# The first products of two MLPs by one level of Strassen's algorithm, and the hidden tiles in four batches of eight

## The chip, the core and the metric

The kernel runs on one core of a Trainium2 chip. The metric is the time of one execution on the device in microseconds (us). The kernel before was timed three times: 1258.25, 1260.36 and 1261.16 us, median 1260.36. One more execution was profiled; the profile and the trace that are quoted here are of that one.

The engines are named as in the profile: PE is TensorE, which multiplies matrices, and PEld its loads of weights; DVE is VectorE, ACT is ScalarE, POOL is GpSimd, and SP is SyncE, which issues nearly all transfers from memory.

## What is computed

Two residual layers on 512 tokens of 1024 features, in float32. Each layer is a mixer (layer 0: convolution and a gated recurrence; layer 1: an attention without softmax) and an MLP with 4096 hidden features. The change touches the MLPs alone; this is the end of each layer in the reference:

```python
shift1, scale1, gate1, shift2, scale2, gate2 = jnp.split(mod[:, None, :], 6, axis=-1)
...
x = x + gate1 * y
h = rms_norm(x, norm_mlp[layer]) * (1.0 + scale2) + shift2
x = x + gate2 * (jnp.square(jax.nn.relu(h @ mlp_w1[layer])) @ mlp_w2[layer])
```

`mod` is the product of a vector with `ada_w` (the "adaLN" numbers: 6 x 1024 for each layer). The kernel works them out beside the other work, and this matters for the order below.

## The kernel before

**Tiles.** Everything lies with the features on the 128 partitions and the 512 tokens along the row. So `h` is eight tiles of 128 x 512 (`hT`), the hidden layer is 32 such tiles, and the output eight.

**Three matmuls for one.** A float32 number is held as a high part, rounded to the format that TensorE takes (fp32r), and a low part, the rest. `mm3` (L288) multiplies high by high, high by low and low by high: three matmuls for each 128 x 128 block of weights. For h the parts are `hh` and `hl`, for the hidden tiles `hidh` and `hidl`, for weights `whi` and `wlo`. Hidden tiles and weights are split by ScalarE (a cast gives the high part) and VectorE (a difference gives the low one).

**Weights.** One weight tile is 128 x 1024 float32, 512 KB: the eight blocks of one hidden tile, or eight blocks of a second-product tile. `raw_w` (L268) loads it by SP into one of three raw buffers; `split_w` makes the parts in one of four `whi` and four `wlo` buffers. SP takes its transfers in order, each when its buffer is free.

**The MLP** (`mlp`, L1002). The hidden tiles are worked in two halves of sixteen. In each half, sixteen first products (24 matmuls of 512 columns each, then relu, square and split in `relu2`, L1006) are followed by the second product: eight output tiles o, each of two weight tiles (48 matmuls of 512 columns), and `x_add` (L508), which adds the result to x. In the second half the outputs 5, 6 and 7 are done in halves of 256 tokens, and the second part of their sums is left to be done after the loop, beside the next norm. `mlp_head` (L1065) does the first three hidden tiles of an MLP in halves of 256 tokens, since the norm of x, and so h, is ready in halves; for layer 1 a copy of it stands in the code of the attention (L1536 and after).

**Work in the background.** `background(n)` (L450) loads n tiles of `ada_w` through the same raw buffers and multiplies each with the vector on VectorE (`ada_dot`, a row `ascr<-wraw,cb`; I call it a dot). In layer 0's MLP two dots follow each hidden tile from the seventh on, and three each output tile of the first half, until none are left.

**What sets the order.** PE's order is that of the code. In the MLPs a scheduler of the language places the instructions of the other engines, each in one order that is fixed in the program; in the attention, and at the start of layer 1's MLP, a planner in the kernel (`Graph`, L110) does it from estimated times. An engine works its instructions strictly in order: one that waits holds up all behind it.

## Time and profile before

| what | before |
|---|---|
| median of three runs | 1260.36 us |
| the profiled execution | 1262.38 us |
| its span in the profile | 1260.6 us |
| granted TensorE clock, mean | 0.997 |
| matmuls in the trace, all | 6809 |
| of 512 columns with h against whi (L291) | 560 |
| of 512 columns with hidden tiles (by each of L291 to L293, with those of 256) | 576 |
| layer 0's MLP begins at | 268.0 us |

A line of a group reads: code line, engine, operation, result<-operands, shape, number of them, then busy time in us, mean length of one in ns, and after the second bar how long the engine had been idle ahead of them and what ended it. A line of the timeline reads: start in us, length in us, engine, line, operation, what, and in brackets the idle time ahead of it. A line of the windows reads: stretch of time, its length, busy time of PE, PEld, DVE, ACT and POOL with the number of instructions begun or running, then the granted clock, the share of the DMA engines and GB/s. A line of transfers ends with the median time in us from issue to landing. [...]

### The profile page before, as it was taken

Reading aid. Unit: us, or ns where it says so; the run is one execution under the profiler, and the core shown is the slowest. Engines: PE = TensorE matmul, PEld = TensorE weight load, DVE = VectorE, ACT = ScalarE, POOL = GpSimd, SP = SyncE. Lnnn points to the kernel's source line nnn. Section 1 sums busy time; section 2 is a strip of 40 time slices with the busy share of each in tenths; the row PEclk is TensorE's granted clock in tenths of the full one; section 3 lists DMA queues with packets and bytes.
Section 4 is the critical chain, followed back from the end, with each engine's and each line's share of the span. In section 5 each row is a group of like instructions: output and inputs, shape, how many; then the busy total and the mean of one; then the engine's idle time right before and its main releaser. Section 6 shows DMA issues by size and latency. Waiting matters only on the chain.

```text
span 1260.6 us, 17038 instructions
## 1 busy us (share of the span) xinstructions
PE 1240.0 (98%) x6809; PEld 1038.2 (82%) x6809; DVE 716.9 (57%) x1107; ACT 541.8 (43%) x891; POOL 12.2 (1%) x24
## 2 busy tenths in 40 slices
PE   7999999999999999999999999999999999999998
PEld 6788877898878888888987778777988888888888
DVE  8897868576666655433567774669753322333321
ACT  4333233355441143622458755667565421355210
POOL 0000000000000000000200000000000000000000
PEclk9999999999999999999999999999999999999999
DMA  8665443416776667332332213323132233222330
GB/s 301 229 211 169 150 151 100 134 35 214 243 247 227 220 205 233 129 97 88 101 101 68 67 53 99 84 68 101 35 101 90 95 100 101 98 89 97 117 109 25
DMA packets 46606, 163.35 MB, mean 130 GB/s; under 512 B 5296, under 2 KB 6328, under 8 KB 46528
## 3 DMA queue, kind: packets, MB, share of 16 engines
q1 hardware_dynamic: 46384, 161.78, 39.4%
q8 instruction: 53, 0.87, 0.3%
q10 hardware_dynamic: 144, 0.49, 0.1%
q14 instruction: 25, 0.20, 0.0%
HBM read 155.96 MB, written 2.10 MB: 125 GB/s over the span
## 4 chain that ended last, share of the span: by engine, by line
PE 86%; DMA 5%; DVE 5%; ACT 3%; issue 1%; SPq 0%; DVEq 0%; ACTq 0%
PE b L291 20%; PE b L292 20%; PE b L293 20%; DMA wraw<-in_w 4%; PE acc L291 3%; PE acc L293 3%; PE acc L292 3%; PE b L1382 2%; PE b L1403 1%; PE b L1438 1%; PE b L1302 1%; ACT whi L281 1%; DVE wlo L282 1%; DVE ascr L422 1%; PE b L1439 1%; PE b L1440 1%
## 5 line engine op out<-in xcount | busy, mean ns | idle before, releaser
L281 ACT CAST whi<-wraw 128x1024 fp32r<-128x1024 f32 x150 | 157.7, 1053 | 450.2 <-PE b L292 262.8
L282 DVE TENSOR_TENSOR wlo<-wraw,whi 128x1024 fp32r<-128x1024 f32 x150 | 183.4, 1224 | 244.2 <-ACT whi L281 241.4
L291 PE MATMUL b<-hh,whi 128*128 128x512 f32 (+1 forms) x720 | 266.9, 371 | 2.0 <-ACT hh L1262 1.1
L293 PE MATMUL b<-hh,wlo 128*128 128x512 f32 (+1 forms) x720 | 262.3, 365 | 0.0
L292 PE MATMUL b<-hl,whi 128*128 128x512 f32 (+1 forms) x720 | 262.2, 365 | 0.0
L291 PE MATMUL b<-hidh,whi 128*128 128x512 f32 (+1 forms) x576 | 207.5, 360 | 1.6 <-ACT hidh L300 1.6
L292 PE MATMUL b<-hidl,whi 128*128 128x512 f32 (+1 forms) x576 | 207.7, 361 | 1.3 <-DVE hidl L301 1.3
L293 PE MATMUL b<-hidh,wlo 128*128 128x512 f32 (+1 forms) x576 | 207.5, 360 | 0.2 <-DVE wlo L282 0.2
L291 PEld LDWEIGHTS b<-hh,whi 128*128 128x128 f32 x720 | 135.1, 188 | 30.6 <-issue 7.2
L293 PEld LDWEIGHTS b<-hh,wlo 128*128 128x128 f32 x720 | 135.0, 188 | 22.1
L292 PEld LDWEIGHTS b<-hl,whi 128*128 128x128 f32 x720 | 135.1, 188 | 21.6 <-DVE hl L1264 0.5
L422 DVE CUSTOM_DVE_ANT_0 ascr<-wraw,cb 128x1024 bf16<-128x1024 f32 x80 | 97.7, 1222 | 46.5 <-DMA wraw<-in_ada 45.9
L292 PEld LDWEIGHTS b<-hidl,whi 128*128 128x128 f32 x576 | 109.1, 189 | 18.2 <-DVE hidl L301 1.6
L291 PEld LDWEIGHTS b<-hidh,whi 128*128 128x128 f32 x576 | 108.5, 188 | 18.4 <-ACT hidh L300 2.0
L293 PEld LDWEIGHTS b<-hidh,wlo 128*128 128x128 f32 x576 | 108.5, 188 | 16.8 <-DVE wlo L282 0.6
L508 DVE SCALAR_TENSOR_TENSOR x<-b,modc,x 128x512 f32<-128x512 f32 (+1 forms) x70 | 44.8, 641 | 96.1 <-PE b L293 95.9
L1216 DVE TENSOR_TENSOR wlo<-raw,whi 128x1024 fp32r<-128x1024 f32 x33 | 40.3, 1222 | 30.1 <-ACT whi L1215 29.9
L301 DVE TENSOR_TENSOR hidl<-relu,hidh 128x512 fp32r<-128x512 f32 (+1 forms) x64 | 42.4, 665 | 23.4 <-ACT hidh L300 23.2
L291 PE MATMUL acc<-hh,whi 128*128 128x512 f32 x128 | 52.2, 408 | 0.0
L293 PE MATMUL acc<-hh,wlo 128*128 128x512 f32 x128 | 50.0, 390 | 0.0
L292 PE MATMUL acc<-hl,whi 128*128 128x512 f32 x128 | 49.9, 390 | 0.0
L1366 DVE TENSOR_TENSOR_SCAN om<-om,pat 128x772 f32<-128x772 f32 (+2 forms) x24 | 46.5, 1936 | 5.8 <-ACT om L1362 5.8
(335 smaller groups left out, 1783.3 us busy)
## 6 DMA issues: line engine op xcount, KB each, us to landing
wraw<-in_w SPq DMA_DIRECT2D x125, 512.0 KB, 3.6
wraw<-in_ada SPq DMA_DIRECT2D x80, 512.0 KB, 4.4
eraw<-in_ada SPq DMA_DIRECT2D x16, 512.0 KB, 4.8
wraw<-in_win SPq DMA_DIRECT2D x16, 512.0 KB, 3.5
raw<-in_wqk SPq DMA_DIRECT2D x16, 512.0 KB, 3.6
raw<-in_ws SPq DMA_DIRECT2D x8, 512.0 KB, 6.8
wraw<-in_woab SPq DMA_DIRECT2D x8, 512.0 KB, 3.5
raw<-in_wvc SPq DMA_DIRECT2D x8, 512.0 KB, 3.9
```

Source lines behind the costliest of these rows:

```text
L281: act.copy(hi, raw)
L282: dve.tensor_tensor(lo, raw, hi.bitcast(F32), op=ALU.subtract)
L291: pe.matmul(ps, whi, h[0][:, hs], start=start, stop=False)
L292: pe.matmul(ps, whi, h[1][:, hs], start=False, stop=False)
L293: pe.matmul(ps, wlo, h[0][:, hs], start=False, stop=stop)
L301: dve.tensor_tensor(lo[:, sl], t_[:, sl], hi[:, sl].bitcast(F32), op=ALU.subtract)
L422: dve.tensor_tensor_reduce(out=scr, in0=raw, in1=cb, scale=1.0, scalar=0.0, op0=ALU.mult, op1=ALU.add, accum_out=modr[:, col:col + 1])
L508: dve.scalar_tensor_tensor(x[o][:, sl], ps, mcol(l, v, o), x[o][:, sl], op0=ALU.mult, op1=ALU.add)
L1216: on_dve(1024, lambda: dve.tensor_tensor(lo.t, raw.t, hi.t.bitcast(F32), op=ALU.subtract), (raw, hi), (lo,), 1)
L1302: on_pe(0.13, lambda s=s, sq=sqs[p, s, s0]: pe.matmul(ms.t[64 + 32 * s:96 + 32 * s, sl], hs, sq.t[:, sl], start=True, stop=True), (sqs[p, ...
L1366: on_dve(2 * nw, lambda: dve.tensor_tensor_scan(s_(), s_(), pats[i][:, ::-1], 0.0, op0=ALU.mult, op1=ALU.max), (om,), (om,), 2)
L1382: pe.transpose(tp.t[:, o_:o_ + P], be.t[:, w0:w0 + P], ident)
```

## The change

**Pairs.** Two hidden tiles are made together, as a product of a 2 x 2 block matrix (the two tiles, the two halves of the 1024 features) by another (the two halves of the features, the two halves of the tokens). In Winograd's form of Strassen's algorithm this takes seven products of quarters for eight. Each product is four blocks, times three matmuls, of 256 columns: 84 for a pair, where there were 48 of 512 columns.

**Sums of h.** `sums` makes four combinations `t0` to `t3` of quarters of h, each with high and low part (128 x 1024), once for a layer, after the second half of the norm. It needs the unsplit norm, which now stays in a tile `tt`, where it was in two small buffers `nt`.

**Sums of weights.** `pair_w` takes the two raw weight tiles r0 and r1 of a pair. The first is split as it is (`wa`); four sums of 512 columns (s_a, s_b, z_a, z_b, in `tt`) give `wb` and `wc`, which are split like weights; the second half of r1 is split into `wdh`, `wdl`, of which there is one buffer each.

**The products.** They run in the order wa, wb, then the last product of the pair before (`before()`), wb, wa, wc, wc, and the own last one (wd with t3) after the next pair's second, or at once where no pair follows. Copies of partial sums (`kept`, on ScalarE) and three adds into `cm` (on VectorE) put the four quarters together; relu, square and split follow.

**Batches.** The hidden tiles are worked in four batches of eight. The head has four tiles (two pairs' worth), so batch 0 has two pairs more and the others four: 14 pairs a layer. The second product of a batch takes one weight tile for each output (24 matmuls), so x_add runs four times for each output. Two dots follow each output tile until none are left, which is after batch 2 of layer 0; eight are put ahead of output tile 3 of layer 0's projection, where none stood.

The diff, cut to its core:

```diff
+    tt = base.tile([P, NT * T], F32, name="tt")
+    tt3 = tt.rearrange("p (k t) -> p k t", t=T)
+    dsh = base.tile([P, 8], F32, name="dsh")
...
-        t_ = base.tile([P, T], F32, name="nt", tag="nt", bufs=2)
+        t_ = tt[:, tsl(i)]
...
+    background(8)
...
+    def sums(l, th, on):
+        lo_, hi_ = slice(0, 4), slice(4, 8)
+        q = lambda k, hf: tt3[:, k, H[hf]]
+        regs = lambda k, hf: [(i, hf) for i in range(k.start, k.stop)]
+        s2, hd = l * 48 + SHIFT2 * 8, Handle()
+        on("DVE", 8, lambda: dve.tensor_tensor(dsh[:, 4 * l:4 * l + 4], modc[:, s2 + 4:s2 + 8], modc[:, s2:s2 + 4], op=ALU.subtract), [], [hd])
+        view = lambda t_: t_.rearrange("p (k t) -> p k t", t=256)
+        def high(i, k, hf):
+            on("ACT", 1024, lambda: act.copy(view(th[i][0].t), q(k, hf)), regs(k, hf), [th[i][0]])
+        def low(i, k, hf):
+            on("DVE", 1024, lambda: dve.tensor_tensor(view(th[i][1].t), q(k, hf), view(th[i][0].t).bitcast(F32), op=ALU.subtract),
+               regs(k, hf) + [th[i][0]], [th[i][1]])
+        def less(out, a, sh, b):
+            for j in range(4):
+                (ko, fo), (ka, fa), (kb, fb) = [(k + j, hf) for k, hf in (out, a, b)]
+                on("DVE", 310, lambda ko=ko, fo=fo, ka=ka, fa=fa, kb=kb, fb=fb, j=j: dve.scalar_tensor_tensor(
+                    q(ko, fo), q(ka, fa), sh(j), q(kb, fb), op0=ALU.add, op1=ALU.subtract), [(ka, fa), (kb, fb), hd], [(ko, fo)])
+        on("DVE", 1024, lambda: dve.tensor_tensor(q(lo_, 0), q(lo_, 1), q(lo_, 0), op=ALU.subtract), regs(lo_, 0) + regs(lo_, 1), regs(lo_, 0))
+        high(0, lo_, 0)
+        less((0, 1), (4, 1), lambda j: dsh[:, 4 * l + j:4 * l + j + 1], (0, 1))
+        low(0, lo_, 0)
+        shift = lambda j: mcol(l, SHIFT2, 4 + j)
+        less((0, 0), (4, 1), shift, (0, 0))
+        high(1, lo_, 0)
+        less((4, 0), (4, 0), shift, (0, 0))
+        low(1, lo_, 0)
+        high(3, hi_, 0)
+        high(2, lo_, 1)
+        low(3, hi_, 0)
+        low(2, lo_, 1)
...
+    def pair_w(l, i, hp):
+        r0, r1 = raw_w(w1_d[l, 2 * i]), raw_w(w1_d[l, 2 * i + 1])
+        a, b = slice(0, T), slice(T, 2 * T)
+        def place():
+            nsum[0] += 1
+            n = (nsum[0] - 1) % 4
+            return tt[:, 1024 * n:1024 * n + 1024]
+        wa, s_ = split_w(r0, None, AT256), place()
+        dve.tensor_tensor(s_[:, a], r1[:, a], r1[:, b], op=ALU.add)
+        dve.tensor_tensor(s_[:, b], s_[:, a], r0[:, a], op=ALU.subtract)
+        wb, z_ = split_w(s_, None, AT256), place()
+        dve.tensor_tensor(z_[:, a], r0[:, b], s_[:, b], op=ALU.subtract)
+        dve.tensor_tensor(z_[:, b], r0[:, a], r1[:, a], op=ALU.subtract)
+        wc = split_w(z_, None, AT256)
+        wd = [hp.tile([P, 576], F32R, name=n, tag=n)[:, 16:528] for n in ("wdh", "wdl")]
+        split(r1[:, b], *wd)
+        return wa, wb, wc, wd
+    def pair(l, i, hp, th, hid, before):
+        wa, wb, wc, wd = pair_w(l, i, hp)
+        a, b, c = [acc(256) for _ in range(3)]
+        cm = [hp.tile([P, T], F32, name="cm", tag="cm", bufs=3) for _ in range(2)]
+        out = [hid_new(hp, 2 * i + j) for j in range(2)]
+        hid += out
+        b11 = [(hT[k], H[0]) for k in range(4)]
+        b21 = [(hT[k], H[0]) for k in range(4, 8)]
+        b22 = [(hT[k], H[1]) for k in range(4, 8)]
+        t1, t2, t3, t4 = [[(t_, slice(256 * k, 256 * k + 256)) for k in range(4)] for t_ in th]
+        def prod(ps, w, at, bs, first):
+            for k, (h, sl) in enumerate(bs):
+                mm3(ps, w, slice(at + k * P, at + (k + 1) * P), h, sl, first and k == 0, k == 3, skip_group_check=True)
+        def kept(ps):
+            t_ = hp.tile([P, 256], F32, name="kept", tag="kept", bufs=5)
+            act.copy(t_, ps)
+            return t_
+        def relu2(j, sl, ps=None):
+            c_ = cm[j][:, sl]
+            act.activation(c_, c_ if ps is None else ps, AF.Relu)
+            act.activation(c_, c_, AF.Square)
+            split(cm[j], *out[j], sl)
+        prod(a, wa, 0, b11, True)
+        p1 = kept(a)
+        prod(c, wb, 0, t1, True)
+        p5 = kept(c)
+        before()
+        prod(a, wb, T, t2, False)
+        u2 = kept(a)
+        prod(b, wa, T, b21, True)
+        dve.tensor_tensor(cm[0][:, H[0]], b, p1, op=ALU.add)
+        prod(c, wc, 0, b22, False)
+        dve.tensor_tensor(cm[0][:, H[1]], c, u2, op=ALU.add)
+        relu2(0, FULL)
+        prod(a, wc, T, t3, False)
+        dve.tensor_tensor(cm[1][:, H[1]], a, p5, op=ALU.add)
+        relu2(1, H[1])
+        def last():
+            prod(a, wd, 0, t4, False)
+            relu2(1, H[0], a)
+        return last
+    def mlp(l, last, hp, head, th):
         nrm = Norm(1, 0, (7,)) if not last else None
-        for hb in range(2):
-            j0 = 0
-            if hb == 0:
-                hid[:3], j0 = head, 3
-            for j in range(j0, 16):
-                w = load_w(w1_d[l, hb * 16 + j])
-                ps = acc()
-                for k in range(NT):
-                    mm3(ps, w, ks(k), hT[k], FULL, k == 0, k == NT - 1)
-                relu2(j, ps)
-                if j > 5:
-                    background(2)
-            hk = list(hid)
-            for o in range(8 if hb == 0 else 5):
-                ps = acc()
-                for c in range(2):
-                    w = load_w(w2_d[l, hb, o, c])
-                    for k in range(8):
-                        mm3(ps, w, ks(k), hk[c * 8 + k], FULL, c == 0 and k == 0, c == 1 and k == 7)
+        for b in range(4):
+            hid, rest = list(head) if b == 0 else [], lambda: None
+            for i in range(len(hid) // 2, 4):
+                rest = pair(l, 4 * b + i, hp, th, hid, rest)
+            rest()
+            for o in range(8 if b < 3 else 5):
+                w, ps = load_w(w2_d[l, b // 2, o, b % 2]), acc()
+                for k in range(8):
+                    mm3(ps, w, ks(k), hid[k], FULL, k == 0, k == 7)
                 x_add(o, ps, FULL, l, GATE2)
-                if hb == 1:
+                if b == 3:
                     if last:
                         sync.dma_start(out_d[o], x[o])
                     else:
                         nrm.add(o, FULL)
-                if hb == 0:
-                    background(3)
+                background(2)
         if not last:
             log_exp_tables()
-        ps, banks = {}, {}
+        ps, banks, ws = {}, {}, []
         for o in range(5, 8):
-            w = load_w(w2_d[l, 1, o, 0], None, AT256)
             for hf in range(2):
                 banks[bank[0] % 8] = o, hf
                 ps[o, hf] = acc(256)
-                for k in range(8):
-                    mm3(ps[o, hf], w, ks(k), hk[k], H[hf], k == 0, False)
-        ws = []
-        for o in range(5, 8):
-            if last or o == 5:
-                ws.append(load_w(w2_d[l, 1, o, 1], None, AT256))
-                continue
-            raw, j = raw_w(w2_d[l, 1, o, 1]), 2 * (o - 6)
-            parts = [[hp.tile([P, T], F32R, name=n, tag=f"{n}{j + i}") for i in range(2)] for n in ("hidh", "hidl")]
-            for i in range(2):
-                split(raw[:, i * T:(i + 1) * T], parts[0][i], parts[1][i])
-            ws.append((Joined(parts[0]), Joined(parts[1])))
-        return nrm, ps, banks, hk[8:], ws
+            ws.append(load_w(w2_d[l, 1, o, 1], None if o == 5 else (hp, f"t{o - 6}h", f"t{o - 6}l"), AT256))
+        return nrm, ps, banks, hid, ws
...
-        w = [load_w(w1_d[l, j], None, AT256) for j in range(3)]
+        w = [load_w(w1_d[l, j], None, AT256) for j in range(4)]
...
+        th = [[Handle(t=hp.tile([P, 1088], F32R, name=f"t{i}{a}", tag=f"t{i}{a}")[:, AT512]) for a in "hl"] for i in range(4)]
+        sums(l, th, lambda eng, n, fn, r, w: fn())
         run(head(1))
-        return hid
+        return hid, [(a.t, b.t) for a, b in th]
...
+    sums(1, th, issue)
...
-    _, ps, _, hk, ws = mlp(1, True, h1, [(a.t, b.t) for a, b in hid])
+    _, ps, _, hk, ws = mlp(1, True, h1, [(a.t, b.t) for a, b in hid], [(a.t, b.t) for a, b in th])
     for hf in range(2):
         for o in range(5, 8):
             for k in range(8):
-                mm3(ps[o, hf], ws[o - 5], ks(k), hk[k], H[hf], False, k == 7)
+                mm3(ps[o, hf], ws[o - 5], ks(k), hk[k], H[hf], k == 0, k == 7)
```

Two places show what becomes of VectorE's order. In the rows, a name with a number is one of several buffers, `b` is a buffer of PSUM, `x` a tile of the residual stream.

The first place is VectorE at the start of layer 0's MLP, from the end of the second half of the norm. Before:

```order
L468 SCALAR_TENSOR_TENSOR nt<-x_67,gsc,ny 128x256
L468 SCALAR_TENSOR_TENSOR nt<-x_68,gsc,ny 128x256
L301 TENSOR_TENSOR hidl<-relu_2458,hidh 128x256
L470 SCALAR_TENSOR_TENSOR hl_2147<-nt,modc,hh_2146 128x256
L470 SCALAR_TENSOR_TENSOR hl_2149<-nt,modc,hh_2148 128x256
L301 TENSOR_TENSOR hidl<-relu_2464,hidh 128x256
L301 TENSOR_TENSOR hidl<-relu_2470,hidh 128x256
L282 TENSOR_TENSOR wlo<-wraw,whi 128x1024
```

After the last norm tile (hl) and the head's first hidden tiles the next weight's low part comes at once. In the changed kernel one wide difference (L1031) stands ahead of the last two hl, then four sums with `dsh` and two hidl, and then:

```order
L1021 TENSOR_TENSOR t0l<-tt,t0h 128x1024
L291 TENSOR_TENSOR hidl<-cm,hidh 128x256
L1028 SCALAR_TENSOR_TENSOR tt<-tt,modc 128x256 x2
L291 TENSOR_TENSOR hidl<-cm,hidh 128x256
L1028 SCALAR_TENSOR_TENSOR tt<-tt,modc 128x256 x6
L1021 TENSOR_TENSOR t1l<-tt,t1h 128x1024
L1021 TENSOR_TENSOR t2l<-tt,t2h 128x1024
L1021 TENSOR_TENSOR t3l<-tt,t3h 128x1024
L272 TENSOR_TENSOR wlo<-wraw,whi 128x1024
L1058 TENSOR_TENSOR tt<-wraw 128x512
L291 TENSOR_TENSOR hidl<-cm,hidh 128x256 x2
L1059 TENSOR_TENSOR tt<-tt,wraw 128x512
```

All sums of h (L1028) and the four low parts (L1021) now stand ahead of the first pair's first weight (L272, wa), and the sums for its second (L1058 is s_a, L1059 is s_b) behind that, with the hidl of the head's second half between. Layer 1 has the same instructions at its start, with wa's low part and three of the four later hidl ahead of t1l to t3l and s_a.

The second place is VectorE at the end of a batch in layer 0. Before, at the end of the first sixteen hidden tiles:

```order
L422 ISA ascr,modr<-wraw,cb 128x1024
L422 ISA modr 128x1
L301 TENSOR_TENSOR hidl<-relu_3098,hidh 128x512
L422 ISA ascr,modr<-wraw,cb 128x1024
L422 ISA modr 128x1
L282 TENSOR_TENSOR wlo<-wraw,whi 128x1024 x2
L422 ISA ascr,modr<-wraw,cb 128x1024
```

Dots (`ascr`) stand among the low parts of hidden tiles and weights. In the changed kernel, at the end of batch 1, during the products of its last pair:

```order
L291 TENSOR_TENSOR hidl<-cm,hidh 128x512
L291 TENSOR_TENSOR hidl<-cm,hidh 128x256
L291 TENSOR_TENSOR wdl<-wraw,wdh 128x512
L420 ISA ascr,modr<-wraw,cb 128x1024
L420 ISA modr 128x1
L291 TENSOR_TENSOR hidl<-cm,hidh 128x256
L1104 TENSOR_TENSOR cm<-b_3692,kept 128x256
L272 TENSOR_TENSOR wlo<-wraw,whi 128x1024
L1106 TENSOR_TENSOR cm<-b_3693,kept 128x256
L420 ISA ascr,modr<-wraw,cb 128x1024
L420 ISA modr 128x1
L1109 TENSOR_TENSOR cm<-b_3691,kept 128x256
```

The last row is the add that follows the pair's seventh product here called P7. The pair's last product goes on in the buffer that this add reads, so it waits for the add; and ahead of the add now stand wdl, two dots of the second product's phase and a weight's low part (L272). The second of these dots uses the raw buffer that r1 of this pair leaves at wdl. In batch 3 of layer 0 and in layer 1 there are low parts of w2 weights at this place and no dots.

More of the change, by code (lines that the diff above doesn't have):

```diff
@@ new lines, in trunk, with hid_new @@
+    HID = 10
+    def hid_new(hp, j):
+        return tuple(hp.tile([P, T], F32R, name=n, tag=f"{n}{j % HID}") for n in ("hidh", "hidl"))
+    def sums(l, th, on):
[28 more added lines that the diff above has]
+        low(2, lo_, 1)
```

94 lines of the change are left out of this document (42 added, 52 removed).

## The prediction

> **What bounds the kernel now.** I read the page's busy shares first, then its chain that ended last, then single matmuls on the timeline.
>
> ```profile
> span 1260.6 us, 17038 instructions
> PE 1240.0 (98%) x6809; PEld 1038.2 (82%) x6809; DVE 716.9 (57%) x1107; ACT 541.8 (43%) x891; POOL 12.2 (1%) x24
> PE 86%; DMA 5%; DVE 5%; ACT 3%; issue 1%; SPq 0%; DVEq 0%; ACTq 0%
> ```
>
> PE is busy 98% of the span and 86% of the chain. Whatever shortens PE's stream counts in full, as long as VectorE (57%) and ScalarE (43%), which get more to do, still deliver in time. How fast does PE go? Durations overlap, so I take the distance between starts, for matmuls of 512 columns, then of 256 in two places:
>
> ```profile
> 1111.65 0.39 PE L291 MATMUL b<-hh,whi 128*128 128x512 f32 x1
> ...
> 1113.01 0.39 PE L291 MATMUL b<-hh,whi 128*128 128x512 f32 x1
> 923.94 0.28 PE L291 MATMUL b<-hh,whi 128*128 128x256 f32 x1
> ...
> 926.21 0.28 PE L293 MATMUL b<-hh,wlo 128*128 128x256 f32 x1
> 1223.17 0.28 PE L291 MATMUL b<-hidh,whi 128*128 128x256 f32 x1
> ...
> 1225.88 0.28 PE L293 MATMUL b<-hidh,wlo 128*128 128x256 f32 x1
> ```
>
> Six steps of 512 columns take 1.36 us: 0.2267 each. Twenty of 256 take 2.27: 0.1135. In the tail 23 take 2.71: 0.1178. Both are about half of 0.2267, so PE pays for columns, not for instructions. [...]
>
> Where PE does stall in an MLP is instructive, since the change makes more such places (layer 0, from its first sixteen hidden tiles to the second product):
>
> ```profile
> 364.31 1.05 ACT L281 CAST whi<-wraw 128x1024 fp32r<-128x1024 f32 x1 [5.30 <-DMA wraw<-in_w]
> 368.15 0.51 PE L291 MATMUL b<-hidh,whi 128*128 128x512 f32 x1 [1.57 <-ACT hidh L300]
> 369.98 0.80 PE L292 MATMUL b<-hidl,whi 128*128 128x512 f32 x1 [1.33 <-DVE hidl L301]
> 366.00:370.00 4.00, 1.10 (x5) 0.36 (x3) 3.66 (x6) 2.06 (x3) 0.00 (x0) 0.99 0.58 169
> 370.00:374.00 4.00, 4.00 (x11) 3.20 (x12) 2.33 (x4) 0.00 (x0) 0.00 (x0) 0.58 0.92 349
> 362.00:366.00 4.00, 4.00 (x20) 3.30 (x19) 1.85 (x4) 1.68 (x3) 0.00 (x0) 1.00 0.92 332
> ```
>
> A cast of a weight not needed yet waits 5.30 us for its load; the hidden tile's relu stands behind it. PE idles 2.9 of 4 us, and then the granted clock is 0.58: 11 matmuls where 20 stood before, 1.8 us more. So a stall of about 3 us costs 4.7, and I give every stall of that length or more 1.8 us on top. [...]
>
> **The gain.** A pair of hidden tiles takes 48 matmuls of 512 columns now, 48 x 0.2267 = 10.88 us, and then 84 of 256: 84 x 0.1135 = 9.53 or 84 x 0.1178 = 9.90. Three of the seven products read hh/hl, like the fast rows; four read the new t tiles, which no row shows. I take the middle, 0.1155, 9.70 us. There are 14 pairs in a layer (2, 4, 4, 4): 28 x 1.18 = **-33.0** (bounds -27.5 and -37.8). The fourth head tile is the same work in halves. The first part of outputs 5 to 7 goes from 144 matmuls of 256 to 72 of 512: 16.96 - 16.32 = 0.64 a layer, **-1.3**. The stall above goes, since its place is now a batch end, counted below: **-4.7**.
>
> **The load on the other engines.**
>
> ```profile
> L282 DVE TENSOR_TENSOR wlo<-wraw,whi 128x1024 fp32r<-128x1024 f32 x150 | 183.4, 1224 | 244.2 <-ACT whi L281 241.4
> L301 DVE TENSOR_TENSOR hidl<-relu,hidh 128x512 fp32r<-128x512 f32 x58 | 40.0, 690 | 23.2 <-ACT hidh L300 23.0
> L301 DVE TENSOR_TENSOR hidl<-relu,hidh 128x256 fp32r<-128x256 f32 x6 | 2.4, 421 | 0.2 <-ACT hidh L300 0.2
> L422 DVE CUSTOM_DVE_ANT_0 ascr<-wraw,cb 128x1024 bf16<-128x1024 f32 x80 | 97.7, 1222 | 46.5 <-DMA wraw<-in_ada 45.9
> L470 DVE SCALAR_TENSOR_TENSOR hl<-nt,modc,hh 128x256 fp32r<-128x256 f32 x16 | 7.0, 481 | 0.8 <-ACT hh L469 0.8
> L281 ACT CAST whi<-wraw 128x1024 fp32r<-128x1024 f32 x150 | 157.7, 1053 | 450.2 <-PE b L292 262.8 <-DMA wraw<-in_w 111.8 <-PE acc L292 50.7
> L1011 ACT ACTIVATE relu<-relu 128x512 f32<-128x512 f32 x58 | 36.7, 633 | 1.8
> L300 ACT CAST hidh<-relu 128x512 fp32r<-128x512 f32 x58 | 36.0, 621 | 1.8
> L1009 ACT ACTIVATE relu<-b 128x512 f32<-128x512 f32 x58 | 34.3, 591 | 0.7 <-PE b L293 0.7
> L1082 ACT ACTIVATE relu<-relu 128x256 f32<-128x256 f32 x6 | 2.3, 415 | 0.0
> L1080 ACT ACTIVATE relu<-b 128x256 f32<-128x256 f32 x6 | 2.1, 377 | 0.0
> wraw<-in_w SPq DMA_DIRECT2D x125, 512.0 KB, 3.6
> wraw<-in_ada SPq DMA_DIRECT2D x80, 512.0 KB, 4.4
> ```
>
> VectorE, per pair: three low parts of 1024 (3.67), four weight sums, wdl and one hidl of 512 (6 x 0.69 = 4.14), two hidl and three adds of 256 (5 x 0.42 = 2.11): 9.9 us, against 2 x (1.22 + 0.69) = 3.8 now. ScalarE: three casts (3.16), wdh 0.62, three copies (1.13), relu, square and cast of 512 (1.85) and twice of 256 (2 x 1.2): 9.2. Back to back an operation costs some 0.09 us less than its duration (below), so VectorE needs about 8.6 of the pair's 9.7: it just fits. In a steady pair I lay PE out in steps of 1.39 us (with the former pair's last product third) and VectorE's rows on it in their order: the next pair's wb and wc low parts come at 8.1 and 10.1 and are wanted at 11.1 and 16.6. So I take **+2** for all pairs (bounds 0, and 10 if each loses a third of a microsecond). The eight adaLN dots put ahead of output tile 3 of layer 0's projection lie beside its matmuls; I take 0 (1 us if that weight comes late). The four x_adds more per output tile fit beside a second product of 5.44 us.
>
> **The two MLP starts.** The sums that give t0 to t3 stand on VectorE between the last norm tile and the first pair's weights, and nothing on PE covers them but the head.
>
> ```profile
> 267.86 1.22 DVE L282 TENSOR_TENSOR wlo<-wraw,whi 128x1024 fp32r<-128x1024 f32 x1
> 268.99 0.88 DVE L470 SCALAR_TENSOR_TENSOR hl<-nt,modc,hh 128x256 fp32r<-128x256 f32 x2
> ...
> 281.14 0.88 DVE L470 SCALAR_TENSOR_TENSOR hl<-nt,modc,hh 128x256 fp32r<-128x256 f32 x2
> 281.94 0.75 DVE L301 TENSOR_TENSOR hidl<-relu,hidh 128x256 fp32r<-128x256 f32 x2
> 284.99 0.40 PE L291 MATMUL b<-hh,whi 128*128 128x512 f32 x1
> 921.11 0.89 DVE L1264 SCALAR_TENSOR_TENSOR hl<-nt,modc,hh 128x256 fp32r<-128x256 f32 x2 [0.18 <-ACT hh L1262]
> 928.02 0.40 PE L291 MATMUL b<-hh,whi 128*128 128x512 f32 x1
> ```
>
> Back to back a 1024-wide operation costs 1.13 (268.99 - 267.86), a 256-wide one 0.40 with a scalar (0.88 - 0.48) and 0.33 without (0.75 - 0.42), a 512-wide one 0.60. Layer 0: the head of three ends at 284.99; a fourth tile (48 x 0.114 = 5.5) makes it 290.4. The last hl comes at 282.0, and 282.4 with the wide difference ahead of it (one earlier hidl moved behind). Then follow twelve sums of 0.40, four hidl of 0.33 and four low parts of 1.13: 293.0; the low part of wa: 294.2. PE has idled 3.8 us. wb needs s_a and s_b with two hidl between (1.9: 296.1), its cast (297.2), and VectorE, busy with two more sums and two hidl to 298.0: wb is ready at 299.2, when its product should have begun at 291.8. That is 7.4 late, and after two idle stretches of 3.5 us and more the half clock takes 1.8: +9.2. Layer 1: the same list, with eight hidl, wa and two sums ahead of s_b, from about 920.5: 1.1 + 4.8 + 2.6 + 4.5 + 1.1 + 1.8 = 16 us, 936.6; cast and low part make 938.9. By before's rows four tiles are done at 928.02 plus six more matmuls, 929.4, and wb is wanted at 930.8: 8.1 late, 9.9 with the half clock. Both: **+19** (bounds 15, without half clock, and 21).
>
> **The batch ends.** Once a batch's pairs are through, PE wants the last product at once, and it waits for P7's add on VectorE (the order above). In layer 0's first three batches a dot stands before that add. Its load needs the raw slot of r1(3), free after wdl. In the last pair's frame: the former pair's last product ends at 4.2, wdh 4.8, wdl 5.5, the load lands 4.4 later at 9.9, dot and read-out 1.3, the add 0.4: 11.7, and PE was ready at 9.7: 2.0. The next batch's start pays too, since a weight with two dots behind it turns a raw slot more slowly than PE's 5.44 us:
>
> ```profile
> 295.05 1.05 ACT L281 CAST whi<-wraw 128x1024 fp32r<-128x1024 f32 x1 [2.48 <-DMA wraw<-in_w]
> ...
> 346.92 1.05 ACT L281 CAST whi<-wraw 128x1024 fp32r<-128x1024 f32 x1 [3.75 <-DMA wraw<-in_w]
> ```
>
> Nine casts, eight steps, 51.87 us: 6.48 each. Eight outputs use up 8.3 us of lead; from the first w2 weight at 2.9 the next wa is ready at 54.7, and wb behind three sums, wdl, an x_add and its low part at 59.0, where PE wants it at 58.0: 1.0. So 3.0 at three batch ends. At the other five no dot stands there, and only the add itself and a hop are paid, 0.6. Together 9 + 3 = **+12** (bounds 5, the add alone everywhere, and 34, the rival below).
>
> **The sum.** -33.0 - 1.3 - 4.7 + 2 + 19 + 12 = -6.0. The profiled execution took 1262.38 (its span and 1.8 around it), 2.0 above the median of the three runs shown, 1260.36. So 1256.4 in its terms, **1254.4** in the median's: 0.5% faster.
>
> **Rivals.** (1) The gain arrives nearly whole: 0.1135 for all new products, starts and batch ends at their lower bounds: -37.8 - 1.3 - 4.7 + 0 + 15 + 5 = -24, 1237. For it: the fast rows of hh. Against: VectorE's order at the starts. (2) VectorE sets the pace of a pair: 10.0 us instead of 9.7, 28 x 0.3 = 8 more, 1262, no change that a measurement can tell. For it: 9.9 us of durations; against: back-to-back costs. (3) Slower: the P7 add at a batch end stands behind a load that comes late. VectorE and the loads' queue work in order, so one late weight moves all behind it. Landing 3 us later makes the wait 5.1, with half clock 6.9, at three ends, and a w2 weight ahead of the add 2.6 at five: 33.7 instead of 12, 1276. The stall at 366 is this mechanism at one place. It decides from 8.5 us more, 2.6 us per batch end instead of 1.5. Against it: slots are handed to the earliest free. [...] That the change doesn't reduce PE's columns can't be: the order shows 84 matmuls of 256 columns for 48 of 512.
>
> **How the numbers follow.** The forecast gets 0.50, (1) 0.11, (2) 0.12, (3) 0.26, (4) 0.01. Under 0.2% (2.5 us) a measurement of this kernel can't tell a difference. Of the forecast 0.44 lies below 1257.8 and 0.06 above; of (2) 0.08 is the same and 0.04 slower. Faster 0.55, same 0.14, slower 0.31. The range reaches from (1) to (3): 1236 to 1278; the forecast's own is 1243 to 1264.
>
> **What would show it.** Starts: PE idle near 290 and 931 in two stretches, with the clock at half behind them. Batch ends: PE's last products waiting for an add behind a dot. Pairs: starts 9.7 us apart; if 9.5 or 9.9, the cadence was off. Gaps at every pair would speak for (2), half clock at several batch ends for (3). A sum that is wrong by more than 20 us means a wait that I haven't seen.

## The result, and the profile after

| | median us | lowest to highest | runs |
|---|---|---|---|
| before | 1260.49 | 1258.25 to 1262.72 | 5 |
| changed | 1273.30 | 1269.31 to 1274.86 | 5 |

The changed kernel takes 1.0094 of the time before, with a 95% interval from 1.0068 to 1.0119: 0.9% slower, where 0.5% faster was forecast. The profiled execution of it took 1269.31 us, the shortest of its five, and that of before 1262.38, so the two traces show 6.9 us of the 12.8 between the medians.

The page of the changed kernel, with the span, the busy line and the chain by engine:

```profile
span 1267.5 us, 19414 instructions
PE 1224.1 (97%) x7721; PEld 1069.3 (84%) x7721; DVE 904.9 (71%) x1455; ACT 622.9 (49%) x1127; POOL 13.8 (1%) x24
PE 78%; DVE 12%; DMA 5%; ACT 3%; issue 2%; SPq 0%; DVEq 0%; ACTq 0%
```

PE is busy for 15.9 us less than before (1240.0), and yet the span is 6.9 us longer: PE waits more. VectorE has gone from 5% of the chain to 12%. Whom PE waits for stands in the view of waits of the changed kernel (total us, times, longest us):

```profile
PE b L281 <- DVE cm L1109: 11.0, 8, 2.5
PE b L281 <- ACT whi L271: 6.4, 2, 4.4
PE b L281 <- DVE x L506: 6.1, 3, 3.0
PE b L283 <- DVE wlo L272: 3.2, 4, 1.6
```

The first row is the batch ends, eight of them; the second and the fourth are the starts of the two MLPs. All three are in the forecast. The third, PE waiting for an x_add, is not. The same view of before has little of it:

```profile
PE b L291 <- DVE x L508: 1.0, 2, 0.8
```

Where in the program the time went is read best from PE's own rows. Three places occur in both kernels: the end of layer 0's projection (before its MLP), the end of layer 0's MLP, and the first product of layer 1's attention. The timeline of before, then of the changed kernel:

```profile
266.52 0.28 PE L293 MATMUL acc<-yy,wlo 128*128 128x256 f32 x1
...
624.52 0.28 PE L293 MATMUL b<-hidh,hidl 128*128 128x256 f32 x1
...
653.79 0.28 PE L1438 MATMUL b<-whi,hh 128*128 128x256 f32 x1
...
1256.97 0.28 PE L293 MATMUL b<-hidh,wlo 128*128 128x256 f32 x1
```

```profile
262.88 0.28 PE L283 MATMUL acc<-yy,wlo 128*128 128x256 f32 x1
...
624.88 0.28 PE L283 MATMUL b<-hidh,wlo 128*128 128x256 f32 x1
...
659.25 0.28 PE L1521 MATMUL b<-whi,hh 128*128 128x256 f32 x1
...
1263.91 0.28 PE L283 MATMUL b<-hidh,wlo 128*128 128x256 f32 x1
```

Layer 0's MLP: 358.0 us before, 362.0 after. The norm between the layers, which the change was said not to touch: 29.3 and 34.4. The rest with layer 1's norm and MLP: 603.2 and 604.7. Nothing is gained in either MLP as measured from outside, and 5.1 us are lost where no product has changed.

What happens there is VectorE's order. Its timeline before, at the norm between the layers:

```profile
621.88 0.94 DVE L1260 SCALAR_TENSOR_TENSOR nt<-x,gsc,ny 128x256 f32<-128x256 f32 x2
622.74 0.51 DVE L1239 TENSOR_TENSOR nss<-nss,nsq 128x256 f32<-128x256 f32 x1
623.17 0.47 DVE L508 SCALAR_TENSOR_TENSOR x<-b,modc,x 128x256 f32<-128x256 f32 x1
623.57 0.86 DVE L1264 SCALAR_TENSOR_TENSOR hl<-nt,modc,hh 128x256 fp32r<-128x256 f32 x2
...
625.55 0.47 DVE L508 SCALAR_TENSOR_TENSOR x<-b,modc,x 128x256 f32<-128x256 f32 x1
```

and in the changed kernel:

```profile
622.54 1.66 DVE L1343 SCALAR_TENSOR_TENSOR tt<-x,gsc,ny 128x256 f32<-128x256 f32 x4
624.13 1.67 DVE L1347 SCALAR_TENSOR_TENSOR hl<-tt,modc,hh 128x256 fp32r<-128x256 f32 x4
625.71 1.67 DVE L1343 SCALAR_TENSOR_TENSOR tt<-x,gsc,ny 128x256 f32<-128x256 f32 x4
627.30 1.66 DVE L1347 SCALAR_TENSOR_TENSOR hl<-tt,modc,hh 128x256 fp32r<-128x256 f32 x4
...
629.22 0.86 DVE L506 SCALAR_TENSOR_TENSOR x<-b,modc,x 128x256 f32<-128x256 f32 x2
```

Before, the eight norm tiles of the first half of the tokens go two at a time, since `nt` has two buffers, and between the pairs VectorE takes the x_adds and the sums of squares (nss) of the second half as PE delivers them. With eight places in `tt` nothing holds the norm tiles back. All eight run first, and the last two x_adds begin 6.7 us after the first norm tile (622.54 to 629.22), where the last one before began 3.7 us after it (621.88 to 625.55). The norm of the second half needs them and comes late. Four of its casts (hh) then run on ScalarE just ahead of the attention's squares (nsq, L1376) for which PE waits; in before the first four were done by 634.8 us. PE stands for 2.2 us there, where before had a wait of 0.2 us:

```profile
636.22 1.70 ACT L1345 ACTIVATE hh<-tt,modc 128x256 fp32r<-128x256 f32 x4
639.72 1.33 PE L1385 MATMUL b<-nsq,cons 128*32 128x256 f32 x4 [2.24 <-ACT nsq L1376]
```

Behind it the granted clock is 0.73 from 636 to 644 us and 0.84 from 644 to 652; before had 1.00 in both.

### The profile page after: what moved, and what is told of

Read it like the earlier page. It is cut to its first block, busy times and chain, and to the rows that moved or that the text cites. A ratio compares the mean times of both kernels' runs of the same rounds, so it can differ in the third digit from the quotient of the medians.

```text
span 1267.5 us, 19414 instructions
## 1 busy us (share of the span) xinstructions
PE 1224.1 (97%) x7721; PEld 1069.3 (84%) x7721; DVE 904.9 (71%) x1455; ACT 622.9 (49%) x1127; POOL 13.8 (1%) x24
## 4 chain that ended last, share of the span: by engine, by line
PE 78%; DVE 12%; DMA 5%; ACT 3%; issue 2%; SPq 0%; DVEq 0%; ACTq 0%
PE b L281 17%; PE b L283 17%; PE b L282 17%; DMA wraw<-in_w 3%; PE acc L281 3%; PE acc L283 3%; PE acc L282 3%; DVE wlo L272 3%; PE acc L652 2%; PE b L1486 1%; PE b L1465 1%; PE b L1521 1%; ACT whi L271 1%; PE b L1385 1%; PE b L1522 1%
## 5 line engine op out<-in xcount | busy, mean ns | idle before, releaser
L271 ACT CAST whi<-wraw 128x1024 fp32r<-128x1024 f32 x123 | 127.8, 1048 | 238.7 <-DMA wraw<-in_w 103.8
L281 PE MATMUL b<-hh,whi 128*128 128x256 f32 (+1 forms) x624 | 191.7, 307 | 6.2 <-DVE x L506 5.9
L272 DVE TENSOR_TENSOR wlo<-wraw,whi 128x1024 fp32r<-128x1024 f32 x123 | 150.4, 1223 | 61.4 <-ACT whi L271 59.5
L283 PE MATMUL b<-hh,wlo 128*128 128x256 f32 (+1 forms) x624 | 187.2, 300 | 1.9 <-DVE wlo L272 1.9
L282 PE MATMUL b<-hl,whi 128*128 128x256 f32 (+1 forms) x624 | 186.5, 299 | 0.0
L506 DVE SCALAR_TENSOR_TENSOR x<-b,modc,x 128x512 f32<-128x512 f32 (+1 forms) x102 | 68.8, 675 | 105.9 <-PE b L283 105.7
L281 PEld LDWEIGHTS b<-hh,whi 128*128 128x128 f32 x624 | 119.1, 191 | 18.3 <-issue 7.2
L283 PEld LDWEIGHTS b<-hh,wlo 128*128 128x128 f32 x624 | 118.9, 190 | 6.4 <-DVE wlo L272 2.3
L272 DVE TENSOR_TENSOR wlo<-tt,whi 128x1024 fp32r<-128x1024 f32 x56 | 68.3, 1221 | 18.6 <-ACT whi L271 17.7
L271 ACT CAST whi<-tt 128x1024 fp32r<-128x1024 f32 x56 | 57.3, 1050 | 48.6 <-PE b L282 34.1
```

The source lines that it names most:

```text
L271: act.copy(hi, raw)
L272: dve.tensor_tensor(lo, raw, hi.bitcast(F32), op=ALU.subtract)
L281: pe.matmul(ps, whi, h[0][:, hs], start=start, stop=False, **kw)
L282: pe.matmul(ps, whi, h[1][:, hs], start=False, stop=False, **kw)
L283: pe.matmul(ps, wlo, h[0][:, hs], start=False, stop=stop, **kw)
L506: dve.scalar_tensor_tensor(x[o][:, sl], ps, mcol(l, v, o), x[o][:, sl], op0=ALU.mult, op1=ALU.add)
```

## The experiments

My theory after the result: the loss is this order, three times (once for layer 0's MLP, once between the layers, once for layer 1's MLP), and the MLPs themselves do about what was forecast. The rival: the starts and the batch ends cost more than forecast (rival 3 of the prediction). All ratios below are to runs of the kernel before on the same chip; 0.1% is 1.26 us.

| run | median us | ratio | 95% interval |
|---|---|---|---|
| changed | 1273.30 | 1.0094 | 1.0068 to 1.0119 |
| b_nt8 | 1274.33 | 1.0103 | 1.0083 to 1.0122 |
| b_dma | 1260.84 | 0.9999 | 0.9986 to 1.0011 |
| a_plan | 1266.74 | 1.0046 | 1.0031 to 1.0062 |
| a_order | 1268.06 | 1.0056 | 1.0036 to 1.0076 |
| a_plain | 1262.27 | 1.0022 | 1.0006 to 1.0037 |
| a_ends | 1279.07 | 1.0156 | 1.0131 to 1.0180 |
| a_ends2 | 1269.32 | 1.0065 | 1.0048 to 1.0082 |
| a_kick | 1275.59 | 1.0126 | 1.0102 to 1.0151 |
| a_best | 1262.06 | 1.0015 | 0.9998 to 1.0032 |
| a_pp | 1257.01 | 0.9965 | 0.9955 to 0.9975 |
| a_best2 | 1251.71 | 0.9924 | 0.9908 to 0.9940 |
| a_best3 | 1250.51 | 0.9917 | 0.9901 to 0.9933 |

The same three places as above, in the profiled executions (us from one to the next, the last column up to the last matmul of layer 1's MLP):

| run | layer 0's MLP | norm between | to the end |
|---|---|---|---|
| before | 358.0 | 29.3 | 603.2 |
| b_dma | 359.3 | 29.3 | 603.0 |
| b_nt8 | 360.6 | 34.7 | 608.4 |
| changed | 362.0 | 34.4 | 604.7 |
| a_plan | 364.3 | 29.2 | 605.4 |
| a_plain | 359.9 | 34.9 | 597.7 |
| a_ends | 369.7 | 34.4 | 604.8 |
| a_ends2 | 360.4 | 34.4 | 604.5 |
| a_pp | 360.0 | 29.2 | 598.4 |
| a_best2 | 351.1 | 29.2 | 598.0 |

Each row is a single execution. In layer 0's MLP b_dma, which differs from before by that area alone, stands 1.3 us off it, and a_plan, whose edit lies behind that place, 2.3 us off the change. Differences of that size in the first column show nothing.

**b_nt8: the order of the norm alone.** The kernel before, with eight buffers for `nt` at its three places and nothing else of the change. The memory for them is taken from an area for transfers, and b_dma is the kernel before with only that area cut.

```diff
-        t_ = base.tile([P, T], F32, name="nt", tag="nt", bufs=2)
+        t_ = base.tile([P, T], F32, name="nt", tag="nt", bufs=8)
...
-        nts = Ring(lambda k: base.tile([P, T], F32, name="nt", tag="nt", bufs=2), 2)
+        nts = Ring(lambda k: base.tile([P, T], F32, name="nt", tag="nt", bufs=8), 8)
...
-... ring(base, [P, T], F32, "nt", 2) ...
+... ring(base, [P, T], F32, "nt", 8) ...
```

> The kernel before, with one edit: the normed tiles nt get eight buffers instead of two, as the tile tt gives them in the changed kernel (the scratch for transfers is made smaller to make room, as there). No Strassen, no sums, no new batches. Theory A (order of the norms): with eight buffers the first half's eight norm tiles run ahead of the x_adds and squares that the second half's norm waits for, at three norms, 5.1 + 5.1 + 4.7 = 14.9 us by the milestones of the two traces, so 1270 to 1277. Theory B (the new waits in the pairs, starts and batch ends make the whole loss): the buffers change nothing, 1258 to 1263.

> The kernel before with only the smaller scratch for transfers that b_nt8 and the changed kernel have. Both theories: no change, 1258 to 1263. If it is slower, neither b_nt8 nor the change can be read without it.

More buffers make the kernel before 1.0% slower, as much as the whole change does; the area costs nothing. VectorE of b_nt8 between the layers, and PE's largest wait in it:

```profile
623.23 1.80 DVE L1260 SCALAR_TENSOR_TENSOR nt<-x,gsc,ny 128x256 f32<-128x256 f32 x4
...
630.18 0.87 DVE L508 SCALAR_TENSOR_TENSOR x<-b,modc,x 128x256 f32<-128x256 f32 x2
```

```profile
PE b L291 <- DVE x L508: 8.0, 3, 4.6
```

It is the order of the changed kernel, without any of Strassen's products. By the table of places it costs 2.6 + 5.4 + 5.2 = 13.2 us in the profiled executions. The norm between the layers and that of layer 1's MLP pay clearly; for layer 0's MLP the 2.6 is little above the spread, but PE's wait for x at its start is 3.2 us, and 0.8 in before and in b_dma. So the theory holds for the kernel before. How much of the change's own loss this is, the next runs have to show.

**a_plan, a_order: the old order in the changed kernel.** In a_plan the planner sees a ring of two that has no memory behind it, so norm tiles go two at a time again between the layers and in layer 1. a_order also issues the first half's norm tiles of layer 0 in pairs, 2 us apart.

```diff
+    nts = Ring(lambda k: None, 2)
...
-            t_, g, sh = tth[i][hf], ...
+            n_, t_, g, sh = nts.new(), tth[i][hf], ...
...
-                   ...), (xh[i, hf], y), (t_,), 0)
+                   ...), (xh[i, hf], y), (t_, n_), 0)
```

> The changed kernel; at the two norms that the planner orders (between the layers, and layer 1's MLP) a norm tile waits for the last but one before it, as the two buffers made it do. All else stays. Theory A: 5.1 + 4.7 = 9.8 us come back, about 1263. Theory B: 1273 as it was.

> As a_plan, and at the norm of layer 0's MLP the first half's norm tiles are issued in pairs 2 us apart instead of all at once, so that x_adds come between. Theory A: another 3 to 5 us, about 1259, the same as the kernel before or a little below. Theory B: 1273 as it was.

a_plan takes 0.48% off, and the norm between the layers is back at 29.2 us. The last part is not: 605.4 us, as in the change. PE still waits there for the sum of squares, as its row in the view of waits of a_plan shows:

```profile
PE b L1333 <- DVE nss L1323: 3.8, 1, 3.8
```

So the expectation was too high: in layer 1 one wait has taken the place of another (in the change PE waits there 3.05 us for an x_add and 0.87 for nss). The sums of h on VectorE aren't what makes it, since a_pp, where they come later, has the same 3.8. PE's own order has changed, too: between the attention's last matmul and the first one that takes nss, PE has 33 matmuls of the MLP's head in before (903.86 to 907.48 us), 15 in b_nt8 and only 9 in the change, in a_plan and in a_pp. With 24 more ahead of it, PE would come to that place some 2.7 us later (24 x 113 ns), so this is part of the 3.8. No run gives the head's matmuls their old order; why the planner places them so, and the rest of the wait, are open. a_order adds nothing. In its trace PE's wait for x at the start of layer 0's MLP is 3.2 us, no shorter than in the change (2.9), so the edit didn't restore the order there, and for layer 0 the cure wasn't tried in effect.

**a_plain: cover for the two starts.** Hidden tiles 4 and 5 are done by plain products in both layers, and the sums of h come behind them in the program.

```diff
+            if b == 0:
+                for j in (4, 5):
+                    w, ps = load_w(w1_d[l, j]), acc()
+                    for k in range(NT):
+                        mm3(ps, w, ks(k), hT[k], FULL, k == 0, k == NT - 1)
...
+                sums(l, th, lambda eng, n, fn, r, w: fn())
```

> The changed kernel with the third pair of hidden tiles (4 and 5, the first pair behind the head) in both layers done without Strassen's scheme, as 48 products of 512 columns instead of 84 of 256, and the sums of the activations for the other pairs moved behind it in program order. Its price is 48 x 226.7 ns - 84 x 117.8 ns = +1.0 us a layer. Theory (at the start of both MLPs TensorE waits for VectorE, which has the sums of activations and the new weights to do at the same time: 6.5 us in layer 0 and 6.9 us in layer 1 by TensorE's rows, with half clock behind the stalls): 10.9 us of plain products hide nearly all of it, and the time goes from 1273 to 1259-1265 us (-13.4 of stalls, +2.0 of products, 1-3 left over). Rival (VectorE is short of time in these stretches as a whole, since it also carries the norm's second half; then its late finish only moves to the next pair): less than 4 us, 1269-1275 us.

0.72% less than the change, near the middle of what was expected. PE's waits for whi are gone from its list, and the last part falls by 7.0 us to 597.7. Layer 0's MLP falls by only 2.1 us, within the spread: its waits for cm at the batch ends, 7.9 us in the change, are 9.8 here, so part of the gain only moved there.

**a_ends, a_ends2: dots away from the batch ends.** a_ends takes three dots after the third and each later output tile in place of two after each. a_ends2 takes none after the first, two after the others, and one each behind two of the pairs (one in the first batch).

```diff
-                background(2)
+                background(3 if o > 1 else 0)
```

```diff
                 rest = pair(l, 4 * b + i, hp, th, hid, rest)
+                if i in (1, 2) and b < 3:
+                    background(1)
...
-                background(2)
+                if o:
+                    background(2)
```

> The changed kernel with one number altered: in the second products of a batch, the queued pieces of other work on VectorE and ScalarE are taken 3 at a time, but only after the third and later tiles, where it was 2 at a time after each tile. Theory (the idle of 2.3 to 2.5 us at the ends of three batches of layer 0, for cm L1109, comes from those pieces standing ahead of that add on VectorE, and the idle also brings half clock for about 3 us of the stretch that follows): the waits for cm at 318.9, 406.3 and about 494 us fall to about 0.7 us each, the granted clock there stays at 1, and the time goes from 1273 to 1264-1268 us (3 x 1.7 of idle and 3 x about 1.2 of clock), 1.003-1.006 of the kernel before. Rival (the late add is due to the batch's own sums and weights, not to those pieces; then they only move): waits stay at 2.3-2.5 us and the time stays at 1271-1275 us.

> The changed kernel with the queued pieces of other work moved in another way: none after the first second product of a batch, two after each later one as in the change, and one each behind the second and third pair of hidden tiles, where the transfers and the ring of weight buffers have room. Theory (in a_ends the waits for cm went as expected, but three pieces in a row stood ahead of the weights in the ring of three raw buffers and made those late by more than was gained): the waits for cm L1109 fall from 11.0 us to about 7 as in a_ends, no new waits for whi and wlo appear at the start of the batches, and the time goes from 1273 to 1264-1268 us. Rival (VectorE, busy 87 to 95 per cent in the pairs, has no room for two more pieces of 1.2 us; then the pairs stall): 1270-1277 us.

a_ends is slower than the change by 0.6%, although it does at the batch ends what it was made for. Its waits of PE:

```profile
PE b L281 <- ACT whi L271: 11.3, 7, 4.2
PE b L281 <- DVE cm L1109: 6.7, 8, 1.2
PE b L283 <- DVE wlo L272: 6.3, 9, 1.9
```

The wait for cm falls from 11.0 to 6.7 us, but those for whi and wlo grow by 4.9 and 3.1. SP's queue, VectorE and PE of a_ends at the start of the second batch show why:

```profile
355.73 5.50 SPq L260 DMA_DIRECT2D wraw<-in_ada  x3
362.05 9.77 SPq L260 DMA_DIRECT2D wraw<-in_w  x4
```

```profile
367.83 1.23 DVE L272 TENSOR_TENSOR wlo<-wraw,whi 128x1024 fp32r<-128x1024 f32 x1 [1.73 <-ACT whi L271]
367.85 0.38 PE L281 MATMUL b<-hh,whi 128*128 128x256 f32 x1 [1.64 <-ACT whi L271]
```

Three dots' loads stand in a row in the queue and hold all three raw buffers, and the next weight's load goes out only at 362.05. Its cast and its low part come when PE stands already, and layer 0's MLP takes 369.7 us. a_ends2 is 0.29% below the change, less than expected, and the two intervals overlap, so alone it shows no gain. The waits for cm are 11.6 us in its one trace, no less than in the change.

**a_kick: is the spacing a state that an odd matmul switches?** A plain fp32 matmul of 64 columns after the first product of each batch's first pair.

```diff
         prod(a, wa, 0, b11, True)
+        if first:
+            pe.matmul(acc(64), ones, ones[:, :64], start=True, stop=True)
```

> The changed kernel with eight additional matmuls, one in each batch: a plain fp32 product of 64 columns into a bank of its own, behind the first product of the batch's first pair of tiles. Nothing reads it. Theory (the spacing of the 256-column products, 117.8 ns in some stretches and 113.4 ns in others with the same instructions, is a state of TensorE that a different matmul switches over and that then lasts until the next 512-column stretch): most pairs run at 113.4 ns, 28 x 84 x 4.4 ns x the share of about 0.7 that is at 117.8 now = -7 us, less 8 x 0.3 us, so 1267-1270 us, and the pairs' rows show 113.4. Rival (the spacing is set by something else, such as which buffers are read, and the switch after an odd matmul was chance): spacing unchanged, 1273-1276 us.

No gain. PE of a_kick around the added matmul (L1098), and the last one before its next gap:

```profile
1019.74 0.33 PE L1098 MATMUL b<-ones 128*128 128x64 f32 x2
...
1020.09 0.28 PE L282 MATMUL b<-t0l,whi 128*128 128x256 f32 x1
...
1056.60 0.28 PE L283 MATMUL b<-t2h,wlo 128*128 128x256 f32 x1
```

Between the last two rows lie 310 steps: 117.8 ns each, as in most pairs without the added matmul (about 21 of the change's 28). This is one of its eight places, and the median is 1275.59 us, where the theory put 1267 to 1270. The theory falls.

**a_best to a_best3 and a_pp: edits together.** a_pp is a_plan and a_plain; a_best adds a_ends to them, a_best2 a_ends2, and a_best3 starts the MLPs' PSUM buffers at number 4.

```diff
-    bank = [0]
+    bank = [4]
```

> Three edits at once on the changed kernel: the planner's rule for two norm tiles at a time (as in the run a_plan), the queued work kept off the batch ends (as in a_ends), and the first pair behind the head done plainly in both layers (as in a_plain). If the three losses are separate (6.6 us measured for the first, 5-9 and 8-14 expected for the others): 1246-1254 us, faster than the kernel before by 0.5 to 1.1 per cent. Rival (they are one shortage of VectorE's time that moves from place to place): no better than the best of the three alone, 1260-1267 us.

> Two edits at once on the changed kernel: the planner's rule for two norm tiles at a time (as in a_plan, measured -6.6 us) and the third pair of hidden tiles done plainly (as in a_plain, measured -11.0 us). If these two losses are separate: 1253-1258 us, faster than before by 0.2 to 0.6 per cent. Rival (one shortage of VectorE's time at the start of the second MLP is behind both): 1259-1263 us.

> All three edits: a_plan, a_plain and a_ends2. If a_ends2 takes its 5 to 9 us and the losses are separate: 1246-1252 us, faster than before by 0.6 to 1.1 per cent. If a_ends2 gives nothing, as a_pp: 1253-1258 us.

> As a_best2, and in addition the first tiles of the first MLP take PSUM banks 4 to 7 instead of 0 to 3, so that their products need not wait for the last x_add of the projection (2.9 us in the change, with half clock behind it). Theory: TensorE starts the second of these tiles at once, and the time falls by 2 to 4 us against a_best2. Rival (the low part of the next weights, wlo, which stands behind that x_add on VectorE, ends 1.5 us later and is waited for instead): 0 to 1 us less.

a_plan and a_plain give 0.48% and 0.72% alone and 1.29% together: two separate losses. a_best gives back 0.5% of that through the late weights of a_ends. a_best2 is faster than both kernels, 0.8% below before, and 0.41% below a_pp, with intervals that don't overlap: behind the other two edits a_ends2 does gain. Layer 0's MLP takes 351.1 us in it, where before takes 358.0, and the last part 598.0 for 603.2: now Strassen's products show their gain from outside. a_best3 can't be told from a_best2. PE's wait for x at the start of layer 0's MLP stays at 3.2 us in it, so the edit didn't remove it; why PE waits for that x_add is open.

## Why the prediction was wrong

**The step that failed** is one that the prediction doesn't contain: the move of the norm's tiles from two buffers to eight places was costed at nothing, in the sum and in every rival. The section on the change names that move in a half-sentence, as a matter of memory. b_nt8 shows that in the kernel before it costs 1.03% (interval 0.83 to 1.22), as much as the whole result. In the changed kernel only part of it was taken back: a_plan, at two of the three norms, gained 0.48%, and only the norm between the layers got its old time. If the costs add up, the change without this one would have come out near no difference; no run shows that directly. In the profiled executions: -3.6 us before the projection's end (266.52 to 262.88; no run tested it, and the place moves between executions: PE's wait for x behind it begins at 263.5 in the change, at 264.4 in a_ends and at 265.4 in a_best2, whose edits lie behind that place), +13.2 by b_nt8's norms, and the remainder of the +6.9 is -2.6, the MLPs, where -6.0 was forecast. By the medians the MLPs' part is 1273.3 - 1274.3 = -1.0. Neither is clear of the spread.

**The gain, -33.0: too large by 3.** Two stretches of the changed kernel, each given by its first and last row:

```profile
452.93 0.28 PE L281 MATMUL b<-hh,whi 128*128 128x256 f32 x1
...
465.54 0.28 PE L283 MATMUL b<-t3h,wdl 128*128 128x256 f32 x1
...
466.14 0.28 PE L282 MATMUL b<-t1l,whi 128*128 128x256 f32 x1
...
490.41 0.28 PE L283 MATMUL b<-t2h,wlo 128*128 128x256 f32 x1
```

107 steps in 12.61 us are 117.9 ns, 214 in 24.27 are 113.4. Both spacings occur with products of hh and of t alike, so the forecast's middle was a mean of two that are not equally frequent: by such stretches about 21 of the 28 pairs ran at 117.8 ns and 7 at 113.4. That makes 9.81 us for a pair and 28 x 1.07 = -30.0.

**The starts, +19: there, but smaller.** PE of the changed kernel at the second products of the first pairs:

```profile
297.38 0.58 PE L281 MATMUL b<-t0h,whi 128*128 128x256 f32 x1 [1.99 <-ACT whi L271]
...
946.14 0.39 PE L281 MATMUL b<-t0h,whi 128*128 128x256 f32 x1 [4.45 <-ACT whi L271]
```

In layer 0 that product's last matmul starts at 300.82 at half clock (0.50 from 294.99 to 301.82, with steps of 0.21 us), and at full clock without waits it would be through at 294.4, by estimate (24 steps of 117.8 ns from the head's end at 291.6): 6.6 late. In layer 1 it is through at 949.7 for 942.9: 6.8. Together +13.4. That the starts cost this and can be covered is shown for layer 1 by a_plain, which gave 9 us net in all; in layer 0 the gain is within the spread.

**The batch ends, +12: the waits as forecast, with half clock besides.** PE in the first two batches of layer 0, and the granted clock (the column ahead of the last two) around the first three of layer 0:

```profile
318.94 0.58 PE L281 MATMUL b<-t3h,wdh 128*128 128x256 f32 x1 [2.39 <-DVE cm L1109]
406.26 0.38 PE L281 MATMUL b<-t3h,wdh 128*128 128x256 f32 x1 [2.30 <-DVE cm L1109]
```

```profile
316.00:324.00 8.00, 5.61 (x26) 5.01 (x26) 7.04 (x12) 5.27 (x10) 0.00 (x0) 0.79 0.75 254
404.00:412.00 8.00, 5.74 (x24) 4.88 (x25) 7.11 (x13) 5.08 (x10) 0.00 (x0) 0.79 0.76 245
492.00:500.00 8.00, 6.84 (x29) 6.10 (x30) 6.56 (x12) 4.84 (x10) 0.00 (x0) 0.79 0.73 238
```

2.0 was forecast for these, and 0.6 for the other five, where the waits are 0.72 to 0.94 us. But I charged half clock only from a stall of about 3 us, and here it comes behind 2.3 to 2.5: 3 x 0.21 x 8 = 5.0 us. With the 11.0 of the view of waits that is +16. The last section shows a wait of this length without half clock behind it. The extra 1.0 at the next batch's start isn't seen.

**The pairs, and rival (2).** VectorE doesn't set the pace: in a stretch of pairs in layer 1 PE is busy throughout, and VectorE 27.27 of 36 us. In layer 0 it is nearer to it, 31.40 of 34 us from 455 to 489, and PE still works 33.90 of them.

```profile
1012.00:1048.00 36.00, 36.00 (x308) 36.00 (x308) 27.27 (x42) 27.66 (x54) 0.00 (x0) 1.00 0.31 103
```

**The old stall, -4.7,** is gone as forecast: no row of PE with a wait stands between 319 and 406. The terms as measured, -30.0 - 4.7 + 13.4 + 16, with the tail's -1.3 as it was put, make -6.6, against -2.6 in the trace; the 4 us between are not taken apart.

**Rival (3)** came near in time, 1276, and was still not the cause: its late loads at the batch ends are worth 16 us and not 33.7, and a kernel without any batch ends (b_nt8) is as slow.

## What to carry to other kernels

A ring of two buffers is not only memory, it is a rule of order: what is ready is placed in as long a row as there are buffers for it (here three or four norm tiles in a row, where there were two), and the work in between moves behind it (in b_nt8 that costs 1.0%). When a change takes such a ring away, look up in the order of instructions which other instructions stood between its uses, who waits for them, and give that a term of the sum, also where the change's own products don't run. And where queued work is moved away from one wait, count the buffers it holds at its new place: in a_ends three dots in a row held all three raw buffers and cost more (8.0 us of waits for whi and wlo) than the wait that they cured (4.3 us for cm).

## What was not expected of the hardware

The same stream of 256-column matmuls runs at 113.4 or at 117.8 ns, for tens of microseconds at a time. In the change it goes over from 117.8 to 113.4 behind a step of 0.38 us (465.54 to 465.92) and stays at 117.8 behind one of 0.22 us (378.25 to 378.47). In a_ends2 it goes over from 113.4 to 117.8 behind one of 0.22 us (398.44 to 398.66), and in a_kick it is 117.8 behind the odd matmul. Why, and what brings 117.8 back, is open; over 28 pairs it is worth 28 x 84 x 4.4 ns = 10 us.

A wait of 2.3 us was followed by half clock in one place and not in another. In the change the one that ended at 406.26 (2.30 us) was. In a_best2 one of 2.34 us was not:

```profile
485.18 0.38 PE L281 MATMUL b<-t3h,wdh 128*128 128x256 f32 x1 [2.34 <-DVE cm L1109]
```

By the clock record of the change's trace a granted clock of 0.50 begins at 318.88, 407.63, 492.96 and 639.74 us, the first three times for 3.41 us and the last for 6.83. The windows around the two waits, first two of the change and then one of a_best2:

```profile
404.22:407.63 3.41, 1.37 (x11) 1.37 (x12) 3.41 (x8) 2.74 (x6) 0.00 (x0) 1.00 0.77 227
407.63:411.04 3.41, 3.41 (x11) 2.73 (x10) 2.89 (x5) 2.33 (x5) 0.00 (x0) 0.50 0.73 270
```

```profile
480.00:488.00 8.00, 5.66 (x44) 5.25 (x43) 5.44 (x10) 4.63 (x10) 0.00 (x0) 1.00 0.69 240
```

In the change PE idles 2.04 of the 3.41 us up to 407.63 (60%), and then the clock is 0.50. In a_best2 PE idles 2.34 of the 3.41 us that end with its wait at 485.18 (69%), and the clock stays at 1.00. So the share of idle time alone does not tell the two apart: in the 3.41 us ahead of the change's eight stretches of half clock between 260 and 950 us it lies between 47% (291.58 to 294.99) and 85% (943.52 to 946.93). What decides it is left open here.
